# One matmul of 256 columns for the first query tile's two score products, and one more VectorE add per head

## The chip, the cores and the metric

The kernel runs on one core of one Trainium2 chip. The metric is the device time of one execution in microseconds (us). The kernel before takes 883.76 us, the median of three runs (883.75 to 883.88).

A core has engines that run side by side, each through its own queue in program order: TensorE (PE in the profile; its weight loads are shown apart as PEld), VectorE (DVE), ScalarE (ACT), GpSimd (POOL) and SyncE (SP), which here issues the loads of the weights. TensorE writes its results to PSUM, in banks of 512 float32 per partition, and VectorE and ScalarE read them there. Engines wait for each other through semaphores. An instruction that waits holds up all that stands behind it in its own queue.

## The reference

A decoder trunk of two layers over 256 tokens of 1024 channels. Each layer runs two token mixers beside each other, an mLSTM and a sliding-window attention, then an output projection, then a squared-ReLU MLP. The change touches the scores of the attention:

```python
scores = jnp.einsum('bnqhgd,bnkhd->bnhgqk', qb, k_ctx) * (A_HEAD_DIM ** -0.5)
...
logits = jnp.where(valid[None, :, None, None], scores + bias, -jnp.inf)
sink = sinks.astype(jnp.float32).reshape(A_KV_HEADS, A_GROUP, 1)
m = jnp.maximum(jnp.max(logits, axis=-1), sink)
p = jnp.exp(logits - m[..., None])
denom = jnp.sum(p, axis=-1) + jnp.exp(sink - m)
out = jnp.einsum('bnhgqk,bnkhd->bnqhgd', p / denom[..., None], v_ctx)
```

There are 16 query heads and 4 key heads of 64 channels. The window is 128 tokens, so the 256 tokens make two query tiles of 128: the first sees 128 keys, the second all 256.

## The kernel before, in words

**Products in two parts.** Every float32 operand of a large product is split into a rounded part "hi" and a rest "lo". A product of two such operands is three matmuls: hi by hi, lo by hi, hi by lo (lines 220 to 222 and 234 to 236). Weights come in pieces of 128 rows by 1024 columns: SP loads a piece (`raw`), ScalarE rounds it to `hi` (line 152), VectorE subtracts to get `lo` (line 127), and TensorE uses both some slots later.

**Slots.** The order of the work is written out by hand. The program is a list of slots; a slot is some 24 matmuls of 256 columns or 12 of 512. Before a slot's matmuls, side work is emitted: `at` puts it ahead of the slot's hi and lo conversions, `at_late` behind the hi conversions, `at_last` behind all conversions. Each engine's queue then holds its part of that list, in that order. ScalarE and VectorE convert pieces four slots ahead of their use, so they run ahead of TensorE in the list.

**Attention.** For attention a query head holds its 64 hi channels and 64 lo channels in the two halves of the 128 partitions, and a key head holds `kh` (hi, in both halves) and `kl` (lo, in both halves). So one matmul with `kh` gives the hi and lo query parts by the hi keys, and a second with `kl` the rest. For each of the 16 heads, called h0 to h15 here, four steps are placed in the slots of the projections from the mLSTM's queries and keys on:

- `att1` (line 825): TensorE makes the scores in one PSUM bank, 128 columns for the first query tile (lines 830 and 831) and 256 for the second (lines 832 and 833). VectorE adds the bias and takes the maximum in one instruction per tile (lines 837 and 839) and negates the maxima (line 841). ScalarE takes the exponentials with their sums (lines 842 to 844).
- `att2`: VectorE makes the reciprocals of the sums (lines 850 and 851), and GpSimd scales both tiles of `L` by them (lines 852 and 853).
- `att3`: TensorE transposes the three 128x128 blocks of `L` into a bank (line 859), and they are copied to `PT`: on VectorE for h0 and h14 (line 862), on ScalarE for the other heads (line 864).
- `att4`: two heads' products with the values (lines 879 and 880).

`heads_at` gives the slot in which each head's `att1` stands; `att2` follows one slot later and `att3` three. h14's `att3` and h15's `att1` stand in one slot. In that slot ScalarE also rounds a piece and takes a tanh for the mLSTM's queries and keys (`silu`, line 776), and VectorE multiplies by it (line 777) ahead of h15's `att1`. The slot after it ends the projection `gb`: ScalarE takes its four banks out of PSUM with a tanh (line 803), and the next projection, `ga`, writes the same four banks.

Both layers run this code; the second's attention lies 430.7 us behind the first's in the trace.

Of the kernel before, what the change touches and what calls it, by code (L numbers as in the profile page):

```python
# [12 lines left out]
F32R = mybir.dt.float32r  # L13
BF16 = mybir.dt.bfloat16
AF = mybir.ActivationFunctionType
ALU = mybir.AluOpType

P = 128
T = 256
# [23 lines left out]
def trunk(ctx: ExitStack, tc: tile.TileContext, x, norm_mix_g, w_in, conv_w, conv_b, b_igate, b_fgate,  # L43
          mlstm_norm_g, attn_sinks, rel_bias, w_branch_m, w_branch_a, w_out, norm_mlp_g, w_up, w_down,
          final_norm_g, out):
    nc = tc.nc
    const = ctx.enter_context(tc.tile_pool(name="const", bufs=1))
    wp = ctx.enter_context(tc.tile_pool(name="wp", bufs=1))
    act = ctx.enter_context(tc.tile_pool(name="act", bufs=1))
# [7 lines left out]
    def nm(s):  # L57
        n_names[0] += 1
        return f"{s}_{n_names[0]}"
# [4 lines left out]
    def psB():  # L64
        return ps.tile([P, 512], F32, tag="B", bufs=4, name=nm("pb"))
# [4 lines left out]
    def small():  # L70
        return act.tile([P, 8], F32, tag="small", bufs=32, name=nm("sm"))
# [310 lines left out]
    biasT = const.tile([P, 16, T], F32, name="biasT")  # L382
# [209 lines left out]
    def mixer(l, ta, tb):  # L592
        w = w_in[l]
        st = {}
# [34 lines left out]
        after(s_kv + 3, kv_evac)  # L629

        def k_split():
            kh = st["kh"] = act.tile([P, 4, T], F32R, tag="kh", bufs=1, name=nm("kh"))
            kl = st["kl"] = act.tile([P, 4, T], F32R, tag="kl", bufs=1, name=nm("kl"))
            kr = st["kraw"].rearrange("p (a t) -> p a t", a=2)
            for par in range(2):
                src = kr[par * 64 : par * 64 + 64]
                own, oth = slice(par * 64, par * 64 + 64), slice(64 - par * 64, 128 - par * 64)
                khv, klv = (t[:, 2 * par : 2 * par + 2, :] for t in (kh, kl))
                for d in (own, oth):
                    nc.scalar.copy(khv[d], src)  # L640
                    nc.gpsimd.tensor_tensor(klv[d], src, khv[own].bitcast(F32), op=ALU.subtract)
# [19 lines left out]
        for i in range(4):  # L661
            after(s_aq + (4 + i if tails[s_aq] != "k" else 7), lambda i=i: aq_evac(i))
        at(s_aq + 1, k_split)


# [158 lines left out]

        def att1(h):
            g = h // 4
            q, kh, kl = st[("q", h // 8)][:, h % 2 * 4 + h % 8 // 2, :], st["kh"], st["kl"]
            gk = g % 2 * 2 + g // 2
            sp = psB()
            nc.tensor.matmul(sp[:, 0:P], q[:, 0:P], kh[:, gk, 0:P], start=True, stop=False, skip_group_check=True)  # L830
            nc.tensor.matmul(sp[:, 0:P], q[:, 0:P], kl[:, gk, 0:P], start=False, stop=True, skip_group_check=True)
            nc.tensor.matmul(sp[:, P : 3 * P], q[:, P:T], kh[:, gk, :], start=False, stop=False, skip_group_check=True)  # L832
            nc.tensor.matmul(sp[:, P : 3 * P], q[:, P:T], kl[:, gk, :], start=False, stop=True, skip_group_check=True)
            L = act.tile([P, 384], F32, tag="L", bufs=5, name=nm("L"))
            mx, nmx, sm = small(), small(), small()
            sk = sink[:, l, h : h + 1]
            nc.vector.tensor_tensor_reduce(L[:, 0:P], sp[:, 0:P], biasT[:, h, P:T], 1.0, sk, op0=ALU.add,
                                           op1=ALU.max, accum_out=mx[:, 0:1])
            nc.vector.tensor_tensor_reduce(L[:, P:384], sp[:, P:384], biasT[:, h, :], 1.0, sk, op0=ALU.add,
                                           op1=ALU.max, accum_out=mx[:, 1:2])  # L840
            nc.vector.tensor_scalar(nmx[:, 0:2], mx[:, 0:2], -1.0, None, op0=ALU.mult)
            nc.scalar.activation(L[:, 0:P], L[:, 0:P], AF.Exp, bias=nmx[:, 0:1], accum_out=sm[:, 0:1])
            nc.scalar.activation(L[:, P:384], L[:, P:384], AF.Exp, bias=nmx[:, 1:2], accum_out=sm[:, 1:2])
            nc.scalar.activation(sm[:, 2:4], nmx[:, 0:2], AF.Exp, bias=sk)
            st[("att", h)] = (L, sm)
# [9 lines left out]
        def att3(h):  # L855
            L, _ = st[("att", h)]
            tp = psB()
            for j in range(3):
                nc.tensor.transpose(tp[:, j * P : (j + 1) * P], L[:, j * P : (j + 1) * P], ident)  # L859
            PT = act.tile([P, 384], F32, tag="PT", bufs=3, name=nm("PT"))  # L860
            if h in (0, 14):
                nc.vector.tensor_copy(PT, tp[:, 0:384])
            else:
                nc.scalar.copy(PT, tp[:, 0:384])
            st[("att", h)] = PT
# [20 lines left out]
        for h in range(16):  # L886
            at_late(s_qk + heads_at[h], lambda h=h: att1(h))
        steps = [(heads_at[h] + j, 4 - j, f, h) for h in range(16) for j, f in ((1, att2), (3, att3))]
        steps += [(heads_at[h + 1] + 4, 0, att4, h) for h in range(0, 16, 2)]
        for i, _, f, h in sorted(steps, key=lambda t: (t[0], t[1], t[3])):  # L890
# [271 lines left out]
```

## Time and profile before

| | before |
|---|---|
| median of three runs | 883.76 us |
| profiled execution, its own time | 884.32 us |
| its span, first to last instruction | 882.5 us |
| TensorE busy | 868.5 us, 98% of the span |
| VectorE busy | 572.4 us, 65% |
| ScalarE busy | 468.2 us, 53% |
| GpSimd busy | 128.3 us, 15% |
| DMA read | 153.23 MB |

A span is what lies between the first and the last instruction of the profiled execution; 1.8 us of its own time lie around it. Matmuls are pipelined, so the busy time of one is longer than the step from one start to the next; what a matmul costs TensorE is that step. In a row of the timeline stand the start in us from the span's start, the duration in us, the engine, the line of the kernel, the operation, the tiles written and read, the shape and the count, and in brackets the idle time of the engine before it, with the instruction that ended it.

### The profile page before, as it was taken

What the parts mean: (1) busy time and instruction counts of PE and PEld (TensorE: products, weight loads), DVE (VectorE), ACT (ScalarE), POOL (GpSimd) and SP (SyncE); (2) the same over time, 40 slices, a digit from 0 to 9 for tenths busy, and PEclk for the clock granted to TensorE, in tenths of its full rate; (3) what the DMA queues carried; (4) which work ended last, traced back from release to release, by engine and by line L of the source; (5) the groups of instructions that cost most, each with busy time, mean ns of one, the idle gap of its engine ahead of it and who ended that gap; (6) DMA issues with size and microseconds to landing.
All of it is one profiled execution on the core that took longest, in us unless ns stands there. A gap on an engine that the chain in (4) does not pass through costs nothing.

```text
span 882.5 us, 15073 instructions
## 1 busy us (share of the span) xinstructions
PE 868.5 (98%) x5929; PEld 789.6 (89%) x5929; DVE 572.4 (65%) x928; ACT 468.2 (53%) x771; POOL 128.3 (15%) x164
## 2 busy tenths in 40 slices
PE   7999999999999999999999999999999999999996
PEld 5899889999989999998889997999998899999985
DVE  5758879666666654546574788876667764737363
ACT  5657776654355554544355557764634453636352
POOL 1360534120000000000002435322000000000000
PEclk9999999999999999999999999999999999999999
DMA  6875435445556747474655455354564466555621
GB/s 217 288 246 186 144 120 167 141 147 158 177 191 202 248 133 240 133 242 136 219 171 189 149 186 163 109 160 144 148 223 157 146 225 225 194 188 188 194 96 48
DMA packets 50711, 155.28 MB, mean 176 GB/s; under 512 B 7912, under 2 KB 10192, under 8 KB 50640
## 3 DMA queue, kind: packets, MB, share of 16 engines
q1 hardware_dynamic: 49456, 150.69, 52.8%
q0 software_dynamic: 896, 3.17, 1.0%
q8 instruction: 46, 0.75, 0.4%
q10 hardware_dynamic: 288, 0.46, 0.1%
q14 instruction: 25, 0.20, 0.1%
HBM read 153.23 MB, written 1.07 MB: 175 GB/s over the span
## 4 chain that ended last, share of the span: by engine, by line
PE 92%; DVE 3%; issue 2%; ACT 1%; POOL 1%; DMA 0%; POOLq 0%; SPq 0%; DVEq 0%; ACTq 0%
PE pa L220 13%; PE pa L221 13%; PE pa L222 12%; PE pa L235 10%; PE pa L234 10%; PE pa L236 10%; PE pb L235 5%; PE pb L234 5%; PE pb L236 5%; PE pb L859 1%; PE pb L322 1%; PE pb L879 1%; DVE lo L127 1%; PE pb L919 1%; PE pb L832 1%
## 5 line engine op out<-in xcount | busy, mean ns | idle before, releaser
L127 DVE TENSOR_TENSOR lo<-raw,hi 128x1024 fp32r<-128x1024 f32 (+1 forms) x276 | 332.0, 1226 | 137.5 <-ACT hi L152 134.4
L152 ACT CAST hi<-raw 128x1024 fp32r<-128x1024 f32 (+1 forms) x280 | 286.1, 1049 | 184.0 <-PE pa L222 48.1
L234 PE MATMUL pa<-xh,hi 128*128 128x256 f32 x864 | 246.4, 285 | 0.0
L235 PE MATMUL pa<-xl,hi 128*128 128x256 f32 x864 | 242.6, 281 | 0.0
L236 PE MATMUL pa<-xh,lo 128*128 128x256 f32 x864 | 241.7, 280 | 0.0
L234 PEld LDWEIGHTS pa<-xh,hi 128*128 128x128 f32 x864 | 162.7, 188 | 0.9 <-issue 0.3
L235 PEld LDWEIGHTS pa<-xl,hi 128*128 128x128 f32 x864 | 162.9, 189 | 0.3
L236 PEld LDWEIGHTS pa<-xh,lo 128*128 128x128 f32 x864 | 162.8, 188 | 0.0
L220 PE MATMUL pa<-hi,xh 128*128 128x512 f32 (+1 forms) x384 | 149.9, 390 | 1.8 <-ACT xh L541 1.8
L221 PE MATMUL pa<-lo,xh 128*128 128x512 f32 (+1 forms) x384 | 148.1, 386 | 0.5 <-DVE lo L127 0.4
L222 PE MATMUL pa<-hi,xl 128*128 128x512 f32 (+1 forms) x384 | 147.8, 385 | 0.0
L234 PE MATMUL pb<-xh,hi 128*128 128x256 f32 x384 | 107.6, 280 | 0.0
L235 PE MATMUL pb<-xl,hi 128*128 128x256 f32 x384 | 107.6, 280 | 0.0
L236 PE MATMUL pb<-xh,lo 128*128 128x256 f32 x384 | 107.3, 280 | 0.0
L220 PEld LDWEIGHTS pa<-hi,xh 128*128 128x128 f32 x384 | 72.2, 188 | 15.4 <-ACT xh L541 2.0
L222 PEld LDWEIGHTS pa<-hi,xl 128*128 128x128 f32 x384 | 72.1, 188 | 15.4
L221 PEld LDWEIGHTS pa<-lo,xh 128*128 128x128 f32 x384 | 72.2, 188 | 15.2 <-DVE lo L127 1.6
L349 POOL TENSOR_TENSOR sm<-sm,mhalf 128x1 f32<-128x1 f32 x9 | 6.6, 731 | 500.0 <-DVE sm L348 500.0
L235 PEld LDWEIGHTS pb<-xl,hi 128*128 128x128 f32 x384 | 72.3, 188 | 1.8
L234 PEld LDWEIGHTS pb<-xh,hi 128*128 128x128 f32 x384 | 72.2, 188 | 1.7
L236 PEld LDWEIGHTS pb<-xh,lo 128*128 128x128 f32 x384 | 72.3, 188 | 0.0
L220 PE MATMUL pa<-hi,b 128*128 128x512 f32 x124 | 48.8, 394 | 0.0
(210 smaller groups left out, 986.1 us busy)
## 6 DMA issues: line engine op xcount, KB each, us to landing
raw<-in_w_in SPq DMA_DIRECT2D x104, 512.0 KB, 4.5
raw<-in_w_up SPq DMA_DIRECT2D x64, 512.0 KB, 4.7
raw<-in_w_down SPq DMA_DIRECT2D x64, 512.0 KB, 4.3
raw<-in_w_branch_a SPq DMA_DIRECT2D x16, 512.0 KB, 3.5
raw<-in_w_branch_m SPq DMA_DIRECT2D x16, 512.0 KB, 4.1
raw<-in_w_out SPq DMA_DIRECT2D x16, 512.0 KB, 4.5
b<-ed SPq DMA_DIRECT2D x4, 512.0 KB, 5.2
g<-in_mlstm_norm_g POOLq DMA_DIRECT2D x2, 512.0 KB, 5.8
```

The costliest lines, as they stand in the source:

```text
L127: nc.vector.tensor_tensor(lo[:, :n], raw[:, :n], hi[:, :n].bitcast(F32), op=ALU.subtract)
L152: nc.scalar.copy(hi[:, :n], raw[:, :n])
L220: nc.tensor.matmul(b, xh[:, kt, s], wh[:, c], start=first, stop=False)
L221: nc.tensor.matmul(b, xh[:, kt, s], wl[:, c], start=False, stop=False)
L222: nc.tensor.matmul(b, xl[:, kt, s], wh[:, c], start=False, stop=last)
L234: nc.tensor.matmul(o, wh[:, c], xh[:, kt, :], start=first and half == 0, stop=False, skip_group_check=True)
L235: nc.tensor.matmul(o, wh[:, c], xl[:, kt, :], start=False, stop=False, skip_group_check=True)
L236: nc.tensor.matmul(o, wl[:, c], xh[:, kt, :], start=False, stop=last, skip_group_check=True)
L322: nc.tensor.transpose(pt[:, j * P : (j + 1) * P], src[:, j * P : (j + 1) * P], ident)
L832: nc.tensor.matmul(sp[:, P : 3 * P], q[:, P:T], kh[:, gk, :], start=False, stop=False, skip_group_check=True)
L859: nc.tensor.transpose(tp[:, j * P : (j + 1) * P], L[:, j * P : (j + 1) * P], ident)
L879: nc.tensor.matmul(o, va[:, 0, vs], PT[:, 0:T], start=(h0 % 4 == 0), stop=False, skip_group_check=True)
```

## The change

The two tiles `kh` and `kl` become the two halves of one tile `k2`. In `att1` one matmul with 256 moving columns takes the first query tile's hi and lo keys together. It writes its first 128 columns to columns 0 to 127 of the bank and its other 128 to columns 384 to 511, which were not used. VectorE adds the bias to the second part into `L`, in an instruction of its own, and the instruction that takes the maximum adds the first part to that. The second query tile is computed as before. Apart from that, h14's copy of `PT` moves from VectorE to ScalarE.

```diff
         def k_split():
-            kh = st["kh"] = act.tile([P, 4, T], F32R, tag="kh", bufs=1, name=nm("kh"))
-            kl = st["kl"] = act.tile([P, 4, T], F32R, tag="kl", bufs=1, name=nm("kl"))
+            k2 = st["k2"] = act.tile([P, 2, 4, T], F32R, tag="k2", bufs=1, name=nm("k2"))
+            kh, kl = k2[:, 0], k2[:, 1]
...
-            nc.tensor.matmul(sp[:, 0:P], q[:, 0:P], kh[:, gk, 0:P], start=True, stop=False, skip_group_check=True)
-            nc.tensor.matmul(sp[:, 0:P], q[:, 0:P], kl[:, gk, 0:P], start=False, stop=True, skip_group_check=True)
-            nc.tensor.matmul(sp[:, P : 3 * P], q[:, P:T], kh[:, gk, :], start=False, stop=False, skip_group_check=True)
-            nc.tensor.matmul(sp[:, P : 3 * P], q[:, P:T], kl[:, gk, :], start=False, stop=True, skip_group_check=True)
+            nc.tensor.matmul(sp.rearrange("p (a t) -> p a t", a=4)[:, 0:4:3, :], q[:, 0:P], k2[:, :, gk, 0:P],
+                             start=True, stop=True, skip_group_check=True)
+            nc.tensor.matmul(sp[:, P : 3 * P], q[:, P:T], k2[:, 0, gk, :], start=False, stop=False, skip_group_check=True)
+            nc.tensor.matmul(sp[:, P : 3 * P], q[:, P:T], k2[:, 1, gk, :], start=False, stop=True, skip_group_check=True)
...
-            nc.vector.tensor_tensor_reduce(L[:, 0:P], sp[:, 0:P], biasT[:, h, P:T], 1.0, sk, op0=ALU.add,
+            nc.vector.tensor_tensor(L[:, 0:P], sp[:, 384:512], biasT[:, h, P:T], op=ALU.add)
+            nc.vector.tensor_tensor_reduce(L[:, 0:P], sp[:, 0:P], L[:, 0:P], 1.0, sk, op0=ALU.add,
                                            op1=ALU.max, accum_out=mx[:, 0:1])
...
-            if h in (0, 14):
+            if h == 0:
                 nc.vector.tensor_copy(PT, tp[:, 0:384])
             else:
                 nc.scalar.copy(PT, tp[:, 0:384])
```

Line numbers from 838 on are one higher in the changed kernel. Below is what stands in the queues at three places, of before first and of the change second.

VectorE, at the first head's `att1` (`b` and `m` are the mLSTM's gate tiles, `pb` the bank of scores, `ISA` the add with maximum and the read of its accumulator; a row names in brackets the engines it waits for):

```order
L713 SCALAR_TENSOR_TENSOR b_160_958<-b_160_958,m_161_988 4x128 [waits DVE_49]
L837 ISA L_1027,sm_1028<-pb_1022,biasT,sink 128x128 [waits PE_49]
L837 ISA sm_1028 128x1
L839 ISA L_1027,sm_1028<-pb_1022,biasT,sink 128x256
L839 ISA sm_1028 128x1
L841 TENSOR_SCALAR sm_1029<-sm_1028 128x2 [waits DVE_49]
```

```order
L713 SCALAR_TENSOR_TENSOR b_159_957<-b_159_957,m_160_987 4x128 [waits DVE_49]
L837 TENSOR_TENSOR L_1025<-pb_1021,biasT 128x128 [waits PE_49]
L838 ISA L_1025,sm_1026<-pb_1021,L_1025,sink 128x128 [waits DVE_49]
L838 ISA sm_1026 128x1
L840 ISA L_1025,sm_1026<-pb_1021,biasT,sink 128x256
L840 ISA sm_1026 128x1
L842 TENSOR_SCALAR sm_1027<-sm_1026 128x2 [waits DVE_49]
```

One instruction is new, and the one behind it waits for it, on the same engine. The same holds for all 32 heads.

ScalarE, in the slots of h13's and h14's `att3` (`hi` is a rounded piece of weights, `PT` a copy of transposed blocks, `b` of lines 771 and 776 the mLSTM's queries and keys, `b` of line 803 the gate):

```order
L864 COPY PT_1976<-pb_1972 128x384
L152 CAST hi_1978<-raw_1770 128x1024
L152 CAST hi_2022<-raw_1831 128x1024
L776 ACTIVATE tmp_2025<-b_222_1332 128x512
L842 ACTIVATE L_2033,sm_2036<-L_2033,sm_2035 128x128
L843 ACTIVATE L_2033,sm_2036<-L_2033,sm_2035 128x256
L844 ACTIVATE sm_2036<-sm_2035,sink 128x2
L771 ACTIVATE b_222_1332<-b_221_1331,cw 128x256
L152 CAST hi_2076<-raw_1903 128x1024
L803 ACTIVATE b_377_2109<-pa_1671 128x512
```

```order
L865 COPY PT_1975<-pb_1971 128x384
L152 CAST hi_1977<-raw_1769 128x1024
L865 COPY PT_2019<-pb_2015 128x384
L152 CAST hi_2021<-raw_1830 128x1024
L776 ACTIVATE tmp_2024<-b_221_1331 128x512
L843 ACTIVATE L_2031,sm_2034<-L_2031,sm_2033 128x128
L844 ACTIVATE L_2031,sm_2034<-L_2031,sm_2033 128x256
L845 ACTIVATE sm_2034<-sm_2033,sink 128x2
L771 ACTIVATE b_221_1331<-b_220_1330,cw 128x256
L152 CAST hi_2075<-raw_1902 128x1024
L803 ACTIVATE b_376_2108<-pa_1670 128x512
```

h14's copy now stands between the two roundings, ahead of the tanh of line 776, of h15's exponentials and of the first tanh of `gb`. The program has this place once per layer.

VectorE, in the same slots:

```order
L127 TENSOR_TENSOR lo_1979<-raw_1770,hi_1978 128x1024
L862 COPY PT_2020<-pb_2016 128x384
L777 SCALAR_TENSOR_TENSOR b_222_1332<-tmp_2025,b_222_1332 128x512
L837 ISA L_2033,sm_2034<-pb_2028,biasT,sink 128x128
L837 ISA sm_2034 128x1
```

```order
L127 TENSOR_TENSOR lo_1978<-raw_1769,hi_1977 128x1024
L777 SCALAR_TENSOR_TENSOR b_221_1331<-tmp_2024,b_221_1331 128x512
L837 TENSOR_TENSOR L_2031<-pb_2027,biasT 128x128
L838 ISA L_2031,sm_2032<-pb_2027,L_2031,sink 128x128
L838 ISA sm_2032 128x1
```

The copy is gone from VectorE's queue. What is left ahead of h15's scores is line 777, which reads the tanh of line 776.

## Rows read from the trace of the kernel before

**Rows 1.** The page: busy time and share of the span of each engine, and the granted TensorE clock in 40 slices.

```profile
PE 868.5 (98%) x5929; PEld 789.6 (89%) x5929; DVE 572.4 (65%) x928; ACT 468.2 (53%) x771; POOL 128.3 (15%) x164
PEclk9999999999999999999999999999999999999999
```

**Rows 2.** The timeline of PE: two heads' scores behind each other and the projection's matmul after them, and, earlier, two matmuls of 256 columns in a projection; lines 235 and 236 stand once each between these two.

```profile
98.92 0.22 PE L830 MATMUL pb<-kh,b 128*128 128x128 f32 x1
99.38 0.22 PE L830 MATMUL pb<-kh,b 128*128 128x128 f32 x1
99.84 0.39 PE L220 MATMUL pa<-hi,xh 128*128 128x512 f32 x1
...
76.85 0.28 PE L234 MATMUL pa<-xh,hi 128*128 128x256 f32 x1
77.20 0.28 PE L234 MATMUL pa<-xh,hi 128*128 128x256 f32 x1
```

**Rows 3.** Groups of VectorE's instructions by line and shape: busy us and mean ns of one, then the idle time before them.

```profile
L474 DVE TENSOR_TENSOR X<-X,pa 128x512 f32<-128x512 f32 x12 | 8.2, 682 | 4.1 <-PE pa L222 4.1
L1114 DVE TENSOR_TENSOR X<-X,pb 128x256 f32<-128x256 f32 x2 | 0.8, 414 | 0.0
L547 DVE SCALAR_TENSOR_TENSOR xl<-pb,gcol,xh 128x128 fp32r<-128x128 f32 x16 | 4.5, 345 | 0.4 <-ACT xh L541 0.4
```

**Rows 4.** The timelines of DVE, POOL and PE at the first two heads: h0's reciprocal and h1's add, GpSimd's scaling of h0 and of h1, and TensorE's transposes of h0 (at 86.28 and 87.18) and of h1 (two of three, from 90.72).

```profile
85.07 0.16 DVE L850 TENSOR_TENSOR sm<-sm 128x2 f32<-128x2 f32 x1
85.26 0.17 DVE L851 RECIPROCAL sm<-sm 128x2 f32<-128x2 f32 x1
85.35 0.33 DVE L837 CUSTOM_DVE_ANT_0 L<-pb,biasT,sink 128x128 f32<-128x128 f32 x1
...
86.21 0.92 POOL L853 TENSOR_SCALAR L<-L,sm 128x256 f32<-128x256 f32 x1
88.64 1.96 POOL L853 TENSOR_SCALAR L<-L,sm 128x256 f32<-128x256 f32 x1
...
86.28 0.33 PE L859 MATMUL pb<-ident,L 128*128 128x128 f32 x1
87.18 0.33 PE L859 MATMUL pb<-ident,L 128*128 128x128 f32 x1 [0.57 <-POOL L L853]
90.72 0.44 PE L859 MATMUL pb<-ident,L 128*128 128x128 f32 x2
```

**Rows 5.** The timelines of ACT, DVE, POOL and PE from h9 to h14: ScalarE's wait for TensorE ahead of h9, h9's add, the negated maximum of h10, h10's exponential, VectorE's wait for its sum, h11's add, GpSimd's first block of h11 and last of h12, the last four of TensorE's six transposes of h11 and h12, and h14's scores.

```profile
121.98 0.59 ACT L313 CAST xh<-pb 128x512 fp32r<-128x512 f32 x1 [0.23 <-PE pb L880]
127.92 0.39 ACT L842 ACTIVATE L<-L,sm 128x128 f32<-128x128 f32 x1
...
125.78 0.35 DVE L837 CUSTOM_DVE_ANT_0 L<-pb,biasT,sink 128x128 f32<-128x128 f32 x1
127.49 0.17 DVE L841 TENSOR_SCALAR sm<-sm 128x2 f32<-128x2 f32 x1
129.11 0.16 DVE L850 TENSOR_TENSOR sm<-sm 128x2 f32<-128x2 f32 x1 [0.70 <-ACT sm L844]
129.45 0.35 DVE L837 CUSTOM_DVE_ANT_0 L<-pb,biasT,sink 128x128 f32<-128x128 f32 x1
...
134.67 0.84 POOL L852 TENSOR_SCALAR L<-L,sm 128x128 f32<-128x128 f32 x1 [3.09 <-DVE sm L850]
138.37 1.28 POOL L853 TENSOR_SCALAR L<-L,sm 128x256 f32<-128x256 f32 x1
...
140.34 0.60 PE L859 MATMUL pb<-ident,L 128*128 128x128 f32 x4
140.70 0.31 PE L830 MATMUL pb<-kh,b 128*128 128x128 f32 x1
```

**Rows 6.** The timelines of ACT, DVE and PE around h14's copy and h15's scores, up to the first tanh of `gb` and the first matmul of `ga`; the first two rows are h3's copy and the rounding behind it.

```profile
95.88 0.48 ACT L864 COPY PT<-pb 128x384 f32<-128x384 f32 x1 [0.96 <-PE pb L859]
96.25 1.05 ACT L152 CAST hi<-raw 128x1024 fp32r<-128x1024 f32 x1
...
148.87 2.00 ACT L152 CAST hi<-raw 128x1024 fp32r<-128x1024 f32 x2
150.77 0.62 ACT L776 ACTIVATE tmp<-b 128x512 f32<-128x512 f32 x1
154.65 0.40 ACT L842 ACTIVATE L<-L,sm 128x128 f32<-128x128 f32 x1 [3.25 <-DVE sm L841]
157.15 0.59 ACT L803 ACTIVATE b<-pa 128x512 f32<-128x512 f32 x1
...
152.52 0.56 DVE L862 COPY PT<-pb 128x384 f32<-128x384 f32 x1 [1.33 <-PE pb L859]
152.99 0.68 DVE L777 SCALAR_TENSOR_TENSOR b<-tmp,b 128x512 f32<-128x512 f32 x1
...
158.45 0.28 PE L234 MATMUL pa<-xh,hi 128*128 128x256 f32 x1
```

**Rows 7.** The same three points in the second layer, from the timelines of ACT and PE.

```profile
585.36 0.40 ACT L842 ACTIVATE L<-L,sm 128x128 f32<-128x128 f32 x1 [3.25 <-DVE sm L841]
587.87 0.58 ACT L803 ACTIVATE b<-pa 128x512 f32<-128x512 f32 x1
...
589.16 0.28 PE L234 MATMUL pa<-xh,hi 128*128 128x256 f32 x1
```

More of the change, by code (lines that the diff above doesn't have):

```diff
@@ L826, in att1 @@
             g = h // 4
-            q, kh, kl = st[("q", h // 8)][:, h % 2 * 4 + h % 8 // 2, :], st["kh"], st["kl"]
+            q, k2 = st[("q", h // 8)][:, h % 2 * 4 + h % 8 // 2, :], st["k2"]
             gk = g % 2 * 2 + g // 2
             sp = psB()
-            nc.tensor.matmul(sp[:, 0:P], q[:, 0:P], kh[:, gk, 0:P], start=True, stop=False, skip_group_check=True)
-            nc.tensor.matmul(sp[:, 0:P], q[:, 0:P], kl[:, gk, 0:P], start=False, stop=True, skip_group_check=True)
-            nc.tensor.matmul(sp[:, P : 3 * P], q[:, P:T], kh[:, gk, :], start=False, stop=False, skip_group_check=True)
-            nc.tensor.matmul(sp[:, P : 3 * P], q[:, P:T], kl[:, gk, :], start=False, stop=True, skip_group_check=True)
+            nc.tensor.matmul(sp.rearrange("p (a t) -> p a t", a=4)[:, 0:4:3, :], q[:, 0:P], k2[:, :, gk, 0:P],
+                             start=True, stop=True, skip_group_check=True)
+            nc.tensor.matmul(sp[:, P : 3 * P], q[:, P:T], k2[:, 0, gk, :], start=False, stop=False, skip_group_check=True)
+            nc.tensor.matmul(sp[:, P : 3 * P], q[:, P:T], k2[:, 1, gk, :], start=False, stop=True, skip_group_check=True)
             L = act.tile([P, 384], F32, tag="L", bufs=5, name=nm("L"))
```

## The prediction

> **What bounds the kernel.** I read the page first: TensorE is busy for 98% of the span, at the full granted clock in every slice [rows 1]. So the time is the length of TensorE's queue, plus the places where it waits. The timeline of PE then gives what a piece of that queue costs, as the step from start to start. What decides here are the places where TensorE waits for a head's chain, or nearly does. I looked for them in the timelines of the attention stage, by setting each of TensorE's instructions beside the end of what it needs. There are four of them in each layer: h0's and h1's transposes [rows 4], h12's transposes and h14's scores [rows 5], and the first matmul of `ga` [rows 6].
>
> **The removed matmul.** Two heads behind each other start at 98.92, 99.38 and 99.84: a head's four matmuls cost 0.46 us. Matmuls of 256 columns start every 0.117 us: three steps from 76.85 to 77.20 [rows 2]. Three of them take 0.35, so a head saves 0.107 us; 16 heads save 1.7 a layer and 32 save 3.4. I use the same saving for heads whose scores stand behind transposes.
>
> **The added add, X.** No row shows it. An add of 128x512 takes 682 ns and one of 128x256 with an operand in PSUM 414, so a column costs 1.05 ns, and 128 columns take 414 - 134 = 280 ns [rows 3]. The instruction behind it waits for it. A reciprocal that waits for the sum before it starts 0.03 us after that one's end (85.26 against 85.23), while h1's add, which waits for nothing of VectorE, starts 0.08 before the reciprocal's end at 85.43 [rows 4]. So the dependent add costs X = 0.28 + 0.03 = 0.31, which I take. From below it is 0.28 - 0.08 = 0.20, if the wait costs nothing. From above it is 0.38, the 345 ns of line 547's 128x128 instruction plus 0.03; that one has three operands, so the adds of rows 3 are nearer.
>
> The Trainium skill, "VectorE: DVE Perf Modes", section on the DRAIN you can't avoid, says that a semaphore after each of a chain of Vector instructions costs nothing extra. The 0.03 against -0.08 of rows 4 speaks against it; by that rule X would be the lower end, and the sum that of the first rival below.
>
> **Where X meets TensorE, per layer.** Lateness is TensorE's time after minus before, from the layer's start.
>
> *h0 and h1.* Three heads' scores stand ahead of h0's transposes: -0.32. h0's reciprocal ends at the end of an unbroken run of VectorE, so GpSimd is X = 0.31 later, and TensorE had waited for it already: its last block ended at 87.13, TensorE went on at 87.18 [rows 4], a lag of 0.05. So TensorE stands at +0.31; 0.63 is lost. h1's block ended at 90.60 and comes 2X later, at 91.22. TensorE reaches the transpose that reads it at 90.83, the second from 90.72 (two with an end 0.11 later than one's). With the lag it now starts at 91.27: +0.43.
>
> *h3 to h13.* These are 11 heads: 0.43 - 1.18 = -0.75, if nothing waits. But ahead of h9 ScalarE's queue waits for TensorE (0.23 us at 121.98), so VectorE rides with it there, at 0.43 - 6 x 0.107 = -0.21. h9 and h10 add X each. Of this, VectorE's wait of 0.70 for ScalarE hides a part: h10's exponential started at 127.92, though its maxima were ready at 127.66 and a hand-over takes 0.09. It is later by the larger of X - 0.21 and 2X - 0.21 - 0.17, which is 0.24. From h11's add at 129.45 VectorE runs without a break up to h12's reciprocal, so h12 is late by 0.24 + 2X = 0.86. GpSimd starts h11 and h12 on that chain at 134.67 and ends at 139.65. TensorE reads the last block from 140.56, the third of the four transposes from 140.34 at steps of 0.11 [rows 5]. The cover is 0.91 - 0.05 = 0.86, so TensorE stands at 0.00: the saving of 0.75 is gone too. h14's scores give -0.11 again.
>
> *h14's copy.* On VectorE it waited for TensorE until 152.52. On ScalarE it starts there too, less 0.11, and holds all behind it: h3's copy shows this, which waited 0.96 us for TensorE with a rounding behind it that started 0.37 after the copy did [rows 6]. The rounding that ran from about 149.8, without a wait, now runs behind the copy. From 152.52: 0.37 for the copy, 0.95 for the rounding (half of the step from 148.87 to 150.77), 0.62 for the tanh, and 0.05 until VectorE's product, which so starts at 154.51 instead of 152.99, 1.52 later. Behind that product stands h15's add: + X. ScalarE had been idle for 3.25 us when h15's exponential came at 154.65, and is busy from there to `gb`'s first tanh, which ended at 157.74 and frees the bank that TensorE writes at 158.45 [rows 6]. Cover: 0.71 - 0.05 = 0.66. Lateness: 1.52 + 0.31 - 0.11 - 0.66 = +1.06. With X left open that is 5X - 0.49: h12 is late by 4X - 0.38, and h15's add brings the fifth. The next three tanhs follow ScalarE's pace and their banks are then in time. h15's own 0.107 is swallowed by this wait.
>
> The move takes 0.47 us of copy (152.52 to 152.99) off VectorE, and that gains nothing: the product behind it comes later, not earlier.
>
> **Sum.** From 158.45 on nothing else changes, and the queues run on relative to TensorE. The second layer has the same rows: 3.25 us of idle time ahead of h15, the tanh's end at 588.45 and the matmul at 589.16, again 0.71 [rows 7]. So 2 x 1.06 = 2.1 us. The profiled execution took 884.32 (a span of 882.5 and 1.8 around it) and would take 886.4. It lies 0.56 above the median of 883.76, so I predict 885.9 for the median.
>
> **Rivals.**
>
> 1. *The late chain is covered better; no change.* With X = 0.20, h10 resumes at 0.02, h12 is late by 0.42, and TensorE stands at -0.44 at h12 and -0.55 behind h14. The copy's wait then gives 1.52 + 0.20 - 0.55 - 0.66 = +0.51 a layer: 884.8. It decides below X = 0.275, where a layer's end comes under 0.88. The lag of rows 4 speaks against it. The same size follows if GpSimd scales h12 faster: its last two blocks stretch over 3.2 us, which need not repeat.
>
> 2. *The side queues ride along; faster.* An earlier TensorE also starts VectorE, GpSimd and ScalarE earlier wherever they wait for it, as at 121.98. If that held at h12 and at h14's copy too, neither would hold TensorE, and a layer would end at 0.43 - 13 x 0.107 = -0.96: 881.8, faster by 0.2%; the saving whole is 880.3. It decides where VectorE has 0.75 us of its own waits left between h9's add and h12's sum, and ScalarE 1.3 us between the copy and `gb`. VectorE's 1.33 us of waiting ahead of the copy [rows 6] speaks for it; that its run from h11's add to h12's sum has no break, and that the copy itself waits for TensorE, against it.
>
> 3. *The split output is slow; slower still.* The new matmul writes two runs of 128 columns 384 apart and reads two runs. No row shows such a one. If it took two steps of 0.117, a head would cost 0.47 as before and TensorE would bring nothing to h9: VectorE rides there at +0.43, h12 is late by 0.43 + 0.45 + 0.62 = 1.50, TensorE by 0.64. With no saving behind h14, the end is 1.52 + 0.31 + 0.64 - 0.66 = +1.81 a layer: 887.4. It decides from the first head on, in every `att1`.
>
> The Trainium skill, "PSUM — Partial Sum Buffer", section Specifications (TRN2), says that any non-contiguous access slows matmuls significantly, and gives no figure; that would be this third rival. No run here shows it yet.
>
> 4. *The upper end of X.* At 0.38, h12 is late by 0.38 + 0.76 = 1.14, TensorE stands at 0.28 - 0.11 = 0.17, and the layer ends at 1.52 + 0.38 + 0.17 - 0.66 = 1.41: 886.6.
>
> **Chances and range.** Forecast 0.52, rival 1 0.28, rival 2 0.05, rival 3 0.06, rival 4 0.09. About 0.2% is what a measurement of this kernel can tell from no change: 1.8 us, so faster is below 882.0 and slower above 885.5. The forecast lies 0.4 above that edge, and I give it 8 in 10 to be above. Slower: 0.42 of it, rivals 3 and 4 whole, and a little of the first: 0.58. Faster: 0.06. Same: 0.36. The range takes in rival 1 and rival 4 with some 0.8 below the first, since h12's cover hangs on GpSimd's uneven durations: 884.0 to 887.0.
>
> **What would show it.** In the profile after: steps of about 0.35 us for a head's scores; the add at about 280 ns, its successor starting right behind its end; TensorE waiting at the transposes of h0 for 0.3 and more longer; ScalarE idle ahead of h14's copy and `gb`'s first tanh later than the matmul of `ga` would need, with a wait of TensorE there of about 1 us in each layer. The prediction is wrong if `ga` starts without a wait, if the copy does not hold ScalarE, or if a head's scores still cost 0.46.

## The result and the profile after

The changed kernel takes 886.32 us (median of nine runs, 886.01 to 886.98), the kernel before, run beside it, 883.75 (nine runs, 883.28 to 883.93). The ratio is 1.0029, with a 95% interval of 1.002 to 1.0038: slower by 2.57 us, where 2.1 was forecast (885.9, range 884.0 to 887.0). One run of the kernel before, beside the first experiments, took 2200.8 us, in the slow state, and is left out of the medians below.

The page after. It answers to [rows 1]:

```profile
PE 867.8 (98%) x5897; PEld 788.4 (89%) x5897; DVE 580.5 (66%) x958; ACT 468.9 (53%) x773; POOL 125.8 (14%) x164
PEclk9999999999999999999999999999999999999998
```

TensorE has 32 instructions fewer, and its granted clock reads the same in every slice but the last (8 for 9). VectorE has 32 more for the adds and 2 fewer for the copies, which ScalarE has gained. A page with shares alike says nothing of 2.57 us; the list of TensorE's waits says where they are (waited for, us in total, times, longest us):

```profile
PE pa L234 <- ACT b L803: 2.4, 2, 1.2
PE pb L860 <- POOL L L854: 2.1, 4, 0.6
...
PE pb L860 <- POOL L L853: 0.5, 1, 0.5
```

The first line is new: `ga`'s first matmul waits for `gb`'s first tanh, once per layer, 1.2 us each. The second was a single wait of 0.6 before (line 853 there); now it comes at h0's and at h12's transposes of both layers. The third is at the first of h0's transposes in the first layer, to which TensorE comes earlier.

The timeline of PE at h0's scores, which answers to the first two rows of [rows 2], and at h0's transposes, to the last three of [rows 4]; the first row is a projection matmul ahead of the attention:

```profile
74.46 0.28 PE L234 MATMUL pa<-xh,hi 128*128 128x256 f32 x1
...
75.17 0.28 PE L830 MATMUL pb<-k,b 128*128 128x256 f32 x1
75.28 0.28 PE L832 MATMUL pb<-k,b 128*128 128x256 f32 x1
75.40 0.28 PE L833 MATMUL pb<-k,b 128*128 128x256 f32 x1
75.52 0.28 PE L234 MATMUL pa<-xh,hi 128*128 128x256 f32 x1
...
85.36 0.33 PE L860 MATMUL pb<-ident,L 128*128 128x128 f32 x1 [0.46 <-POOL L L853]
86.26 0.44 PE L860 MATMUL pb<-ident,L 128*128 128x128 f32 x2 [0.58 <-POOL L L854]
```

The counterpart of the first row in the trace before:

```profile
75.68 0.28 PE L234 MATMUL pa<-xh,hi 128*128 128x256 f32 x1
```

From 75.17 to 75.52 a head's scores cost 0.35 us. The stage begins 1.22 us earlier than before (74.46 against 75.68), from differences ahead of it. So lateness below is the start of the same TensorE instruction after minus before, plus 1.22 in the first layer. For the second layer the reference is the last projection matmul ahead of h0's scores, where after stands 0.34 behind before (507.94 against 507.59).

The timelines of ACT, DVE and PE around h14's copy, which answer to [rows 6]; the last row is the second layer's `ga`:

```profile
148.07 1.06 ACT L152 CAST hi<-raw 128x1024 fp32r<-128x1024 f32 x1
151.53 0.48 ACT L865 COPY PT<-pb 128x384 f32<-128x384 f32 x1 [2.41 <-PE pb L860]
151.91 1.05 ACT L152 CAST hi<-raw 128x1024 fp32r<-128x1024 f32 x1
152.86 0.63 ACT L776 ACTIVATE tmp<-b 128x512 f32<-128x512 f32 x1
155.51 0.40 ACT L843 ACTIVATE L<-L,sm 128x128 f32<-128x128 f32 x1 [2.02 <-DVE sm L842]
...
158.02 0.59 ACT L803 ACTIVATE b<-pa 128x512 f32<-128x512 f32 x1
...
153.52 0.69 DVE L777 SCALAR_TENSOR_TENSOR b<-tmp,b 128x512 f32<-128x512 f32 x1 [1.95 <-ACT tmp L776]
154.13 0.28 DVE L837 TENSOR_TENSOR L<-pb,biasT 128x128 f32<-128x128 f32 x1
154.45 0.35 DVE L838 CUSTOM_DVE_ANT_0 L<-pb,L,sink 128x128 f32<-128x128 f32 x1
...
158.66 0.39 PE L234 MATMUL pa<-xh,hi 128*128 128x256 f32 x1 [1.21 <-ACT b L803]
158.89 0.28 PE L235 MATMUL pa<-xl,hi 128*128 128x256 f32 x1
...
590.75 0.39 PE L234 MATMUL pa<-xh,hi 128*128 128x256 f32 x1 [1.21 <-ACT b L803]
```

Read it from the top. ScalarE reaches the copy after 148.07 and stands idle for 2.41 us, because TensorE has not made h14's transposes. The rounding, which had run there before, comes behind the copy, then the tanh, then VectorE's product, which waited 1.95 us for it. h15's add and maximum follow 0.32 apart, the exponential at 155.51, `gb`'s tanh at 158.02, and TensorE's matmul 0.05 after that tanh's end.

### The profile page after: what moved, and what is told of

Its sections match the earlier page's. It is cut to its first block, busy times and chain, and to the rows that moved or that the text cites. A ratio compares the mean times of both kernels' runs of the same rounds, so it can differ in the third digit from the quotient of the medians.

```text
span 884.2 us, 15067 instructions
## 1 busy us (share of the span) xinstructions
PE 867.8 (98%) x5897; PEld 788.4 (89%) x5897; DVE 580.5 (66%) x958; ACT 468.9 (53%) x773; POOL 125.8 (14%) x164
## 4 chain that ended last, share of the span: by engine, by line
PE 90%; DVE 3%; ACT 3%; issue 2%; POOL 2%; DMA 0%; POOLq 0%; SPq 0%; DVEq 0%; ACTq 0%
PE pa L220 13%; PE pa L221 12%; PE pa L222 12%; PE pa L234 10%; PE pa L235 10%; PE pa L236 10%; PE pb L235 5%; PE pb L234 5%; PE pb L236 5%; PE pb L860 1%; PE pb L322 1%; PE pb L880 1%; PE pb L920 1%; POOL L L854 1%; ACT hi L152 1%
```

## The experiments

What is open after this reading: the change does three things, and the wait at `ga` names only the last link. My theory is that the copy's place in ScalarE's queue makes the wait, and that the adds, by way of h0's and h12's chains, take the saving away. Rivals are that VectorE's greater load is the cost, or that the new matmul saves nothing. All times are medians beside runs of the kernel before on the same chip: 884.03 for the copy back, the copy alone, the saving alone and the later copy, 883.84 for the add alone and the last two. A ratio is the one on record, with its 95% interval; it differs by up to 0.0004 from the quotient of these medians.

**The copy back on VectorE.**

```diff
-            if h == 0:
+            if h in (0, 14):
                 nc.vector.tensor_copy(PT, tp[:, 0:384])
```

> The changed kernel with h14's copy back on VectorE, as in the kernel before. Theory (the copy's place in ScalarE's queue is what costs): h15's chain is late by what TensorE is late at h14 (about +0.1 us) plus one added add (0.31), 0.4 in all, less than the 0.66 of cover ahead of ga; so no wait at ga, the layer ends near its start, and the time is 883.3 to 884.3 us. The waits at h0's and h12's transposes stay. Rival (VectorE's longer work is what costs, wherever the copy stands): VectorE gets 0.47 us more per layer on top of the adds, and the time is 886.3 us or more.

Measured: 883.83 us, ratio 1.0 (0.9991 to 1.0009). TensorE's waits in its trace, of the whole span:

```profile
PE pb L860 <- POOL L L854: 2.1, 4, 0.6
...
PE pb L860 <- POOL L L853: 0.5, 1, 0.5
```

No line names L803: the wait at `ga` is gone, and those at h0 and h12 are what they were. VectorE is busy for 581.6 us, 1.1 more than in the changed kernel, and the time is 2.5 us less. VectorE's load is not the cost.

**The copy alone, in the kernel before.**

```diff
-            if h in (0, 14):
+            if h == 0:
                 nc.vector.tensor_copy(PT, tp[:, 0:384])
```

> The kernel before with nothing changed but h14's copy, which goes to ScalarE: old matmuls, no added add. Theory: the product of line 777 comes 1.52 us later, the cover is 0.66, so TensorE waits 0.86 us ahead of ga in each layer, with about 0.1 for the start after the wait: 0.86 to 0.97 a layer, 885.5 to 885.7 us in all. Rival (the adds are what costs, the copy's move is free): 883.8 us, no wait at ga.

Measured: 886.05 us, ratio 1.0025 (1.0015 to 1.0035). The timelines of ACT, DVE and PE at the same place:

```profile
152.27 0.48 ACT L864 COPY PT<-pb 128x384 f32<-128x384 f32 x1 [2.65 <-PE pb L859]
152.65 1.05 ACT L152 CAST hi<-raw 128x1024 fp32r<-128x1024 f32 x1
153.60 0.63 ACT L776 ACTIVATE tmp<-b 128x512 f32<-128x512 f32 x1
...
154.26 0.69 DVE L777 SCALAR_TENSOR_TENSOR b<-tmp,b 128x512 f32<-128x512 f32 x1 [3.38 <-ACT tmp L776]
...
159.08 0.39 PE L234 MATMUL pa<-xh,hi 128*128 128x256 f32 x1 [0.77 <-ACT b L803]
```

From the copy to the product it is 1.99 us (152.27 to 154.26), against 0.47 before (152.52 to 152.99 in [rows 6]): 1.52 more, as worked out. TensorE's `ga` comes 0.93 later than before, counted from h0's transposes, and the matmul behind it 1.04, in both layers. One line of code, with no new work in it, is so worth 2 us. The time lies 0.35 above the range that was expected: some 0.27 because the kernel before took 884.03 here and not 883.76, and the rest because each layer loses 1.04 and not 0.97.

**The saving alone.**

```diff
-            nc.vector.tensor_tensor(L[:, 0:P], sp[:, 384:512], biasT[:, h, P:T], op=ALU.add)
-            nc.vector.tensor_tensor_reduce(L[:, 0:P], sp[:, 0:P], L[:, 0:P], 1.0, sk, op0=ALU.add,
+            nc.vector.tensor_tensor_reduce(L[:, 0:P], sp[:, 0:P], biasT[:, h, P:T], 1.0, sk, op0=ALU.add,
...
-            if h == 0:
+            if h in (0, 14):
```

> The changed kernel with h14's copy back on VectorE and without the added add, so that the first query tile's scores lack the lo key part: the saving of the matmul alone. Theory: the chains of h0, h1 and h12 hold TensorE as far as VectorE does not ride along; h0's wait swallows three heads' savings (0.32 us), the other 13 are kept where h12 is covered: about 1.1 to 1.4 us a layer, 881.0 to 881.6 us. First rival (all is kept): 880.3 us. Second rival (the split output saves nothing, or each wait gives it back): 883.5 us or more.

Measured: 881.28 us, ratio 0.9973 (0.9962 to 0.9983). In the window of the first attention TensorE's waits are:

```profile
PE pb L859 <- POOL L L853: 0.6, 1, 0.6
PE pb L859 <- POOL L L852: 0.3, 1, 0.3
```

Both are h0's: TensorE comes three heads earlier and waits that much longer, 0.3. From h0 to the end of the stage it gains another 1.3 in each layer, and nothing stops it. So the matmul saves what it was said to save: 2.8 us of the 3.4, the rest swallowed at h0 as the theory has it.

**The add alone.**

```diff
-            nc.vector.tensor_tensor_reduce(L[:, 0:P], sp[:, 0:P], biasT[:, h, P:T], 1.0, sk, op0=ALU.add,
+            nc.vector.tensor_tensor(L[:, 0:P], sp[:, 0:P], biasT[:, h, P:T], op=ALU.add)
+            nc.vector.tensor_tensor_reduce(L[:, 0:P], sp[:, 0:P], L[:, 0:P], 1.0, sk, op0=ALU.add,
```

> The kernel before with nothing but an add of 128x128 more on VectorE per head, whose result the maximum's instruction takes in place of the bias, so that the first query tile's scores count twice. Old matmuls, copy on VectorE: the price of X alone, with no saving to set against it. Theory: h0's transposes 0.31 us late, h1's 0.44, h12's chain 0.44 + 0.45 + 0.62 = 1.51 late against 0.86 of cover, so 0.65 there and about 0.1 for starts after waits; h15's chain is 0.65 + 0.31 - 0.66 = 0.30 late at ga and does not hold TensorE again. 0.65 to 0.8 us a layer: 885.1 to 885.6 us. Rival (VectorE is busy for 65% only, so an add of 0.31 us a head is hidden): 883.7 to 884.2 us.

Measured: 885.44 us, ratio 1.0018 (1.0009 to 1.0027). TensorE's lateness steps up twice in each layer: at h0's transposes by 0.30 and 0.32, behind h12's to 0.67 and 0.74, and nowhere else by more than 0.06; at h1 it does not step, though a wait there was expected. The timeline of PE at h12's transposes, first and second layer:

```profile
139.34 1.22 PE L860 MATMUL pb<-ident,L 128*128 128x128 f32 x6
140.32 0.33 PE L830 MATMUL pb<-kh,b 128*128 128x128 f32 x1
...
570.79 1.20 PE L860 MATMUL pb<-ident,L 128*128 128x128 f32 x6
571.76 0.33 PE L830 MATMUL pb<-kh,b 128*128 128x128 f32 x1
```

From the first of the six transposes to the scores it is 0.98 us (139.34 to 140.32), where the trace before has 0.63 (140.07 to 140.70). This wait stands in no list of waits: the trace folds the six into one row, whose busy time has swallowed it. VectorE is busy for 66% of the span here; that is no cover for an add that stands on a chain.

**The copy on ScalarE, but later.** The copy is emitted behind the slot's rounding and the tanh of line 776, ahead of h15's `att1`:

```diff
+            elif h == 14:
+                st["copy14"] = lambda: nc.scalar.copy(PT, tp[:, 0:384])
...
+        at_late(s_qk + heads_at[14] + 3, lambda: st["copy14"]())
```

> The changed kernel with h14's copy on ScalarE still, but behind the rounding of that slot and the tanh of line 776, ahead of h15's exponentials. Theory (what costs is that the copy holds the rounding and the tanh while it waits for TensorE): the product of line 777 comes as early as before or earlier, h15's exponentials too; 883.3 to 884.3 us, like the kernel with the copy back on VectorE, and no wait at ga. Rival (ScalarE's 0.48 us of work more, wherever it stands, is what costs): 885 us or more.

Measured: 883.52 us, ratio 0.9998 (0.9989 to 1.0007). The timeline of ACT, to set beside the one of the changed kernel:

```profile
148.41 2.00 ACT L152 CAST hi<-raw 128x1024 fp32r<-128x1024 f32 x2
150.30 0.63 ACT L776 ACTIVATE tmp<-b 128x512 f32<-128x512 f32 x1
151.87 0.48 ACT L866 COPY PT<-pb 128x384 f32<-128x384 f32 x1 [0.94 <-PE pb L860]
153.80 0.41 ACT L843 ACTIVATE L<-L,sm 128x128 f32<-128x128 f32 x1 [1.45 <-DVE sm L842]
```

ScalarE does the same work as in the changed kernel. The copy still waits for TensorE, 0.94 us, but only h15's exponential stands behind it, and that waits for VectorE anyway. So neither the copy nor ScalarE's 0.48 us is the price; what the copy holds back is.

**The saving where no chain decides.** The merged matmul and the add for the heads in `ONE` alone, the others as before; the copy back on VectorE:

```diff
+ONE = (3, 4, 5, 6, 7, 8, 9, 10, 13, 14, 15)
...
+            one = h in ONE
+            if one:
...
+            else:
+                for i in range(2):
+                    nc.tensor.matmul(sp[:, 0:P], q[:, 0:P], k2[:, i, gk, 0:P], start=i == 0, stop=i == 1,
+                                     skip_group_check=True)
```

> The changed kernel with h14's copy back on VectorE, and with the merged matmul and the added add only for the eleven heads h3 to h10 and h13 to h15; h0, h1, h2, h11 and h12, whose chains TensorE meets, have the matmuls and VectorE instructions of before. Theory (the saving is real, and is lost only where an added add lies ahead of a chain that TensorE waits for): no wait at h1, h12 or ga, eleven heads keep 0.107 us each in both layers, 2.35 us in all: 881.2 to 881.9 us. Rival (VectorE's adds for h9 and h10 still reach h12's transposes, or the saving is lost elsewhere): 883 us or more.

Measured: 881.84 us, ratio 0.9975 (0.9966 to 0.9985). In the window of the first attention one wait of TensorE is left, h0's of before, and at h12 its transposes run through:

```profile
PE pb L868 <- POOL L L862: 0.6, 1, 0.6
...
138.36 0.87 PE L868 MATMUL pb<-ident,L 128*128 128x128 f32 x6
```

The six take 0.87 us, as in the trace before. This kernel is faster than the one before and the changed one: 2.0 us less than before, where eleven heads in two layers at 0.107 would be 2.35. In its trace TensorE gains 1.08 and 1.06 in the two layers, not 1.18. It loses some 0.1 in each at one place, the first projection matmul behind the scores of h5 and h6, which comes up again below.

**The same heads, the copy late on ScalarE.** The last two edits together:

> The same eleven heads, with h14's copy on ScalarE behind the rounding and the tanh. Theory: as with the copy on VectorE, 881.2 to 881.9 us, since neither place then holds anything that TensorE meets. Rival (taking 0.47 us of copy off VectorE gains time of its own): 881.0 us or less.

Measured: 881.74 us, ratio 0.9976 (0.9967 to 0.9985). That is no difference from the kernel with the copy on VectorE: taking the copy off VectorE gains nothing, and costs nothing where it stands well.

## Why the prediction was right, point by point

**The saving, 0.107 us a head.** Shown, by the 0.35 us step and by the kernel without the add. So the third rival, a slow split output, falls: 75.17, 75.28, 75.40 are steps of 0.11 and 0.12, and the two runs of 128 columns cost what one of 256 does. By the rule of the Trainium skill ("PSUM — Partial Sum Buffer", section Specifications (TRN2)) on non-contiguous access, this step should have been slow; here it is not.

**X = 0.31.** The add takes 0.28 and its successor starts 0.32 after it does (154.13 to 154.45). The prediction took the dependent start and not the overlapped one. So it is at 28 of the 32 heads (0.29 to 0.33). At h3 and h4 of both layers, where the successor also waits for a semaphore of GpSimd, the step is 0.42 to 0.44; that is above the prediction's upper end, and it comes back below. By the rule of the Trainium skill on semaphores between Vector instructions ("VectorE: DVE Perf Modes", section on the DRAIN you can't avoid) X would have been 0.20, that of the overlapped start; the trace does not agree.

**h0.** +0.31 was predicted for TensorE, +0.30 and +0.32 are measured in the two layers.

**h1.** This step failed, without weight for the sum: a wait was predicted that takes TensorE to +0.43, and none came; TensorE stays at +0.30 and +0.32. It rested on h1's second block taking 1.96 us on GpSimd, as before. It took 0.93. The timelines of POOL and DVE at this place after:

```profile
88.12 0.93 POOL L854 TENSOR_SCALAR L<-L,sm 128x256 f32<-128x256 f32 x1
...
88.53 1.21 DVE L127 TENSOR_TENSOR lo<-raw,hi 128x1024 fp32r<-128x1024 f32 x1
```

**A place that the prediction did not have.** It named four places in each layer where TensorE meets a chain. There is another: the first projection matmul behind the scores of h5 and h6 (line 220). It needs a bank that ScalarE copies out in line 758, and that copy stands behind h4's exponentials, so behind the adds of h3 and h4. Before, the copy ended at 99.24 and TensorE came at 99.84 [rows 2], so there was cover. The timelines of PEld and PE after, and of PE before:

```profile
98.71 0.19 PEld L220 LDWEIGHTS pa<-hi,xh 128*128 128x128 f32 x1 [0.25 <-ACT b L758]
99.05 0.40 PE L221 MATMUL pa<-lo,xh 128*128 128x512 f32 x1
...
100.06 0.40 PE L221 MATMUL pa<-lo,xh 128*128 128x512 f32 x1
```

TensorE comes to the scores at +0.10 and +0.11. Two savings would take it to -0.11 and -0.10; behind this wait it stands at +0.21 and +0.03. So 0.32 is lost in the first layer and 0.13 in the second. The kernel without the adds loses under 0.03 here and the one with the adds alone 0.06 at most: it takes both, a TensorE that comes earlier and a copy that comes later. In the first layer VectorE's negation of h4's maxima also takes 0.42 us, for 0.17 in the second; why, no run shows.

The loss travels on, since VectorE rides with TensorE ahead of h9, as the prediction has it. ScalarE's row there, which was at 121.98 in [rows 5]:

```profile
120.74 0.59 ACT L313 CAST xh<-pb 128x512 fp32r<-128x512 f32 x1 [0.23 <-PE pb L881]
```

It stands at -0.02 in the first layer and at -0.21 in the second, where -0.21 was forecast. In the second layer two errors cancel: TensorE came 0.11 earlier from h1 than forecast, and lost 0.13 here. In the first layer 0.19 is left, and goes into h12's chain.

**h12.** The chain, not TensorE, sets the time here, as predicted: 0.00 was forecast, +0.14 and -0.05 are measured for the transpose that waits. The 0.19 between the layers is the one from h9. TensorE itself arrived at -0.49 in the first layer and -0.68 in the second, for a forecast of -0.75, and waited. That the sum is this near is luck in part: GpSimd's last block, 1.11 us for 1.28 before, gave back 0.17 that the forecast did not have. The timelines of POOL and PE after, which answer to the last four of [rows 5], and of PE in the second layer:

```profile
138.31 1.11 POOL L854 TENSOR_SCALAR L<-L,sm 128x256 f32<-128x256 f32 x1
...
138.36 0.66 PE L860 MATMUL pb<-ident,L 128*128 128x128 f32 x4
139.48 0.44 PE L860 MATMUL pb<-ident,L 128*128 128x128 f32 x2 [0.47 <-POOL L L854]
139.79 0.36 PE L830 MATMUL pb<-k,b 128*128 128x256 f32 x1
...
570.44 0.66 PE L860 MATMUL pb<-ident,L 128*128 128x128 f32 x4
571.57 0.44 PE L860 MATMUL pb<-ident,L 128*128 128x128 f32 x2 [0.47 <-POOL L L854]
```

**Behind h14's scores.** This is the term that was mis-sized: -0.11 was forecast, +0.18 and 0.00 are measured. The transposes that waited cost more than the wait: from the one that waited to the scores it is 0.31 us (139.48 to 139.79), against 0.14 before (140.56, worked out from [rows 5], to 140.70). With that 0.17, h12's +0.14 and -0.05 and the saving of 0.11 the measured values come out within 0.02. I had priced a wait of TensorE by its length alone.

**h14's copy.** Its mechanism and size are as predicted. From the copy's start to `ga`'s matmul the prediction has 7.10 us (the 5.93 from 152.52 to 158.45 before, and 1.52 + 0.31 - 0.66); measured are 7.13 (151.53 to 158.66). The kernel with the copy alone shows the 1.52 by itself, the kernel with the later copy shows that the rounding and the tanh behind it are what counts.

**The sum.** A layer ends at +1.43 and +1.25 for `ga`'s first matmul, and at +1.54 and +1.36 for the one behind it, where +1.06 was forecast for both. Of the 0.48 and 0.30 too little, 0.29 and 0.11 stood there already behind h14's scores, and 0.11 is the matmul after the wait at `ga`, which the sum again had at no price. What is left is under 0.1. The medians differ by 2.57, the two layers of the profiled executions by 2.9 together. The profiled executions themselves are only 1.69 apart (884.32 and 886.01), as the one after reached the first attention 1.22 earlier; neither lies on its median (883.75 and 886.32).

**The rivals.** The first, a better cover at h12, had its premise half met: GpSimd did scale h12 faster (1.11 us for 1.28), but that gave back 0.17 only, and X was 0.31, where the rival decides below 0.275. The fourth, X = 0.38 for every head, falls by the same rows. The second, side queues that ride along, falls with the waits at h0 and h12. The parts explain the whole: the adds and the saving together are 0 within the interval (the copy back on VectorE), and the copy alone is 2.0. Added up that would be some 1.8 us, short of 2.57. What is missing is the cover: alone, either the copy or h15's add has the 0.66 us ahead of `ga` to itself. Together they have it once, so the add's 0.31 a layer is exposed too. No kernel took only h15's add away, but the two traces with the copy early on ScalarE show it: from the copy's start to `ga`'s matmul it is 6.81 us with the copy alone (152.27 to 159.08) and 7.13 with the adds (151.53 to 158.66). With the 0.11 that h15 saves and the wait swallows, that is 0.43 a layer, and the sum is some 2.7 us.

## What to carry to other kernels

Where one engine is busy for 98% of the span, a saving on it is kept only between the points at which another engine's chain meets it; find those points first, and apply the edit to the work between them. Look too for places with cover that the saving itself uses up, as behind the scores of h5 and h6. An engine's queue is a place, not a load: an instruction that waits costs what stands behind it, so a copy that must wait for TensorE belongs behind the work that need not. Cover is spent once: two delays that each fit under the same slack do not fit together.

## What the runs showed of the hardware

**The first matmul after a wait.** Behind a matmul that waited, the next starts 0.23 us later (158.66 to 158.89), not 0.12. The same 0.11 stands at each `ga` that waited, with and without the adds. A wait of TensorE at such a matmul so costs its length and 0.11 us more; behind the transposes that waited it was 0.17. The weight load of that matmul starts with it, at 158.66, where before it started 0.11 ahead (158.34 for the matmul at 158.45). That this is where the 0.11 comes from is argued; no kernel tested it.

**GpSimd beside VectorE.** A scaling of 128x256 on GpSimd takes 0.92 to 0.93 us by itself. In [rows 4] it took 1.96 from 88.64 on. The timeline of DVE there, in the trace before, has a subtraction of line 127, with two inputs in SBUF, that started 0.03 after it:

```profile
88.67 1.23 DVE L127 TENSOR_TENSOR lo<-raw,hi 128x1024 fp32r<-128x1024 f32 x1
```

After the change the subtraction started 0.41 behind the block, and the block took 0.93. Where the subtraction ran already, as at h2 after the change, the block took 1.66:

```profile
90.80 1.29 DVE L127 TENSOR_TENSOR lo<-raw,hi 128x1024 fp32r<-128x1024 f32 x1 [0.32 <-ACT hi L152]
...
91.23 1.66 POOL L854 TENSOR_SCALAR L<-L,sm 128x256 f32<-128x256 f32 x1
```

The other traces agree: in five of the nine, in both layers, h1's subtraction starts 0.00 to 0.03 behind the block, which takes 1.96 or 1.97, and in the four with the adds of h0 and h1 0.40 or 0.41 behind, and the block takes 0.92 or 0.93. So where the two start, to a few tenths, moves a chain by a microsecond: with VectorE two adds later, h1's scaling ended earlier, not later (89.05 and the 1.22 of the shift are 90.27, against 90.60 before). The Trainium skill, "SBUF — State Buffer", section on the two separate sides, says that VectorE and GpSimd share one pair of ports, and that of a VectorE instruction with two SBUF inputs and a GpSimd one that reads SBUF the one that starts first holds it for its whole instruction. The block of 1.66 us agrees with that. The other two do not, as the trace shows starts: the block of 1.96 us started first, by 0.03, and was held; the subtraction that came 0.41 behind a block was not, with its 1.21 us.
